# Linear attention of the second block's first layer over its context, made in steps between the experts' products

## The chip, the cores and the metric

The kernel runs on one core of a Trainium2 chip. The metric is the device time of one execution in microseconds (us). TensorE does the matrix products, VectorE and ScalarE the elementwise work, GpSimd (POOL) a few fills, and SyncE (SP) issues the large transfers from HBM.

## The reference, cut to what matters

Two transformer blocks run one after the other over 256 latent tokens of 1024 channels, in float32. The first block ends in a mixture of 32 experts. The second block has two layers; in each, the latents (`x`) and 256 context tokens (`ctx`) go through a hybrid mixer: retention and gated linear attention (GLA), each with 4 heads, both directions.

```python
h, hc = modulate_2(rmsnorm(x, ...)), modulate_2(rmsnorm(ctx, ...))
lat, cx = project_in(h, w_in), project_in(hc, w_in)
# GLA, for one direction: context scans from zero, latents from the context's last state
c_f, s_f = chunked_gated_linear_attention(cq, ck, cv, ca_f, zero, False)
x_f, _   = chunked_gated_linear_attention(q, k, v, a_f, s_f, False)
# merge: silu of a gate projection, then w_out and a squared-ReLU MLP, for x and (first layer) for ctx
```

The context of the second block (`ctx_2`) does not depend on the first block. In the first layer its outputs are needed (they go on to the second layer); in the second layer only its last states are.

## The kernel before

Matrix products of the mixers and the MLP split each float32 weight on the chip into a high and a low part: ScalarE rounds a 1 MB chunk to `whi` (`split`, L215), VectorE subtracts it to `wlo` (L216), and TensorE makes three products per tile of 128 x 128 (`mm3`, L226 to L228). The transposed activations stand in `hh` (high parts) and `hl` (low parts), 512 columns wide: columns 0 to 255 are the latents, 256 to 511 the context.

`moe` (the experts) walks over 16 pairs of experts. For each pair `q`, `gate_up` makes gate and up products (L1271) from 8 chunks of 1 MB, and `down` the down products (L1301) of pair `q - 1` from 4 chunks. These products are plain float32, 64 rows of each of two experts side by side in the array. `turned` transposes the hidden layer (L1286). Between the products, `step()` takes pieces from a list: the gathering of rows for the next four experts (`dispatch`, L1234 to L1248) and the adding of results (`combine`, L1319). `weights()` hands out chunks in the order of use, and `chunk(i)` gives each a buffer out of 14: three of the tag `raw` of `s.wp`, three of the tag `raw` of the local pool, the two `whi` and two `wlo` buffers, and four halves of `h0` and `h1`. A chunk's transfer is issued by SP, in order, when the buffer's last product has read it. At the end of `moe`, `context()` loads `ctx_2` and makes its inverse norms.

`block2` then runs the two layers. At the start of a layer, `values` makes the GLA values for all tokens, `proj` the gate's low-rank input, and, for each pair of heads `hp`, keys and queries; a loop over heads makes the decays and the GLA itself. Retention follows (from `vr`, with `proj(512...)`, L1654 on); last come the two gates (`proj_t`, with `sink`, L1733 to L1747), the transposes into `yh`, `yl`, `w_out` and the MLP. In the first layer (`need`), 512 columns are handled throughout; in the second, queries, decays and outputs are 256 wide, but the gate's input, keys and values still 512, and a separate scan (L1564, L1566) makes the context's last states. The modulation vectors of later parts (`ada`, VectorE, L287 and L289) are made in between, a piece at each `tick`.

All engines run their own queues in order. The order in each queue is made when the kernel is built: a planner takes instructions by their place in the program, and moves a ready one ahead of one that it expects to wait; `issue_after` pins a few places. Buffers of a tag are given out as they come free.

## Time and profile before

| what | us |
|---|---|
| median of 3 runs (lowest to highest) | 2022.29 (2019.41 to 2023.18) |
| the profiled execution, its own time | 2024.16 |
| its span, first to last instruction | 2022.0 |
| TensorE busy in the span | 1935.8 |
| VectorE, ScalarE busy | 1136.2, 693.1 |

The experts' stage takes about 415 to 895 us of the span, the first layer of the second block about 895 to 1600 us, and the second layer the rest. "Busy" of TensorE counts modelled ends of pipelined products, so that a high share alone does not say that it runs at its peak; intervals between the starts of like products do. Times are read from one profiled execution.

### The profile page before, as it was taken

The numbers are of one execution on the slowest core, as the hardware profiler recorded it, in microseconds if no ns is written. First come the engines' busy times: TensorE is split into PE (matmuls) and PEld (weight loads), VectorE is DVE, ScalarE is ACT, GpSimd is POOL, SyncE is SP. The second block draws the span as 40 slices with busy tenths as digits, with TensorE's granted clock in tenths as the row PEclk, the third lists the DMA queues.
The fourth block names the chain that finished last, engine by engine and source line by source line (L and its number), as shares of the span: only waits on it lengthen the run. The fifth ranks groups of instructions, "written<-read, shape, count | busy, mean of one in ns | idle before, by whom it ended". The sixth has DMA issues, their size and how long they took to land.

```text
span 2022.0 us, 27853 instructions
## 1 busy us (share of the span) xinstructions
PE 1935.8 (96%) x11540; PEld 1451.0 (72%) x11540; DVE 1136.2 (56%) x2110; ACT 693.1 (34%) x1023; POOL 5.4 (0%) x14
## 2 busy tenths in 40 slices
PE   6998999999999999989899999999999989999998
PEld 2866779844444444357778989778788967988998
DVE  5768795521111111144879959655634667887555
ACT  2564543421111111144432334131323444444444
POOL 0000000000000000000000000000000000000000
PEclk9999999999999999989799999999999989999999
DMA  8436536889999999953133424444423143467553
GB/s 292 161 105 208 167 130 228 310 360 421 420 421 421 421 421 421 421 203 114 43 126 125 148 83 137 155 146 137 134 84 104 56 149 113 151 203 229 176 180 104
DMA packets 218074, 426.15 MB, mean 211 GB/s; under 512 B 16428, under 2 KB 152585, under 8 KB 193113
## 3 DMA queue, kind: packets, MB, share of 16 engines
q1 hardware_dynamic: 208616, 419.75, 57.3%
q10 hardware_dynamic: 9200, 4.51, 0.8%
q8 instruction: 92, 1.51, 0.3%
q14 instruction: 38, 0.30, 0.0%
q0 software_dynamic: 128, 0.08, 0.0%
HBM read 423.26 MB, written 1.05 MB: 210 GB/s over the span
## 4 chain that ended last, share of the span: by engine, by line
PE 66%; DVE 6%; DMA 4%; ACT 2%; issue 1%; DVEq 0%; ACTq 0%; SPq 0%
PE mm L226 14%; PE mm L227 14%; PE mm L228 14%; PE mm L1271 9%; PE mm L1301 3%; PE at L1301 3%; DMA raw<-in_moe_w_down_dram 2%; PE at L1234 2%; PE tr L296 1%; PE at L1319 1%; DMA raw<-in_moe_w_up_dram 1%; DVE wlo L216 1%; DMA rawh<-in_moe_w_gate_dram 1%; DVE sx L1620 1%; DVE acc L289 1%
## 5 line engine op out<-in xcount | busy, mean ns | idle before, releaser
L228 PE MATMUL mm<-hh,wlo 128*128 128x256 f32 (+2 forms) x1232 | 405.7, 330 | 9.2 <-DVE wlo L216 9.2
L226 PE MATMUL mm<-hh,whi 128*128 128x256 f32 (+2 forms) x1232 | 409.9, 333 | 2.8 <-ACT hh L220 1.5
L227 PE MATMUL mm<-hl,whi 128*128 128x256 f32 (+2 forms) x1232 | 407.2, 331 | 0.1
L216 DVE TENSOR_TENSOR wlo<-raw,whi 128x2048 fp32r<-128x2048 f32 (+2 forms) x138 | 303.7, 2200 | 166.0 <-ACT whi L215 165.9
L215 ACT CAST whi<-raw 128x2048 fp32r<-128x2048 f32 (+2 forms) x138 | 253.1, 1834 | 357.9 <-PE mm L227 297.8
L228 PEld LDWEIGHTS mm<-hh,wlo 128*128 128x128 f32 (+1 forms) x1232 | 235.6, 191 | 33.7 <-DVE wlo L216 10.7
L226 PEld LDWEIGHTS mm<-hh,whi 128*128 128x128 f32 (+1 forms) x1232 | 235.6, 191 | 29.3 <-issue 3.6
L227 PEld LDWEIGHTS mm<-hl,whi 128*128 128x128 f32 (+1 forms) x1232 | 235.4, 191 | 25.8 <-issue 5.4
L289 DVE SCALAR_TENSOR_TENSOR acc<-raw,sc,acc 128x512 f32<-128x512 f32 x308 | 218.9, 745 | 14.5 <-DMA raw<-in_ada_w_dram 13.0
L226 PE MATMUL mm<-hidh,whi 128*128 128x256 f32 (+1 forms) x544 | 178.8, 331 | 0.0
L227 PE MATMUL mm<-hidl,whi 128*128 128x256 f32 (+1 forms) x544 | 177.5, 329 | 0.0
L228 PE MATMUL mm<-hidh,wlo 128*128 128x256 f32 (+1 forms) x544 | 177.1, 329 | 0.1
L1271 PE MATMUL mm<-raw,xg 128*64 128x512 f32 x736 | 172.5, 595 | 1.2 <-DMA raw<-in_moe_w_up_dram 1.2
L226 PE MATMUL mm<-whi,hh 128*128 128x256 f32 x512 | 152.9, 299 | 4.7 <-ACT vr L1518 2.9
L227 PE MATMUL mm<-wlo,hh 128*128 128x256 f32 x512 | 151.0, 295 | 3.4 <-DVE wlo L216 3.4
L228 PE MATMUL mm<-whi,hl 128*128 128x256 f32 x512 | 151.7, 297 | 0.7 <-DVE hl L371 0.7
L1271 PEld LDWEIGHTS mm<-raw,xg 128*64 128x64 f32 x736 | 54.6, 137 | 98.0 <-issue 93.0
L1279 DVE SCALAR_TENSOR_TENSOR glo<-mm,ws,glo 128x512 f32<-128x512 f32 x16 | 12.0, 751 | 191.0 <-PE mm L1271 169.0
L227 PEld LDWEIGHTS mm<-hidl,whi 128*128 128x128 f32 x544 | 102.3, 188 | 10.5 <-DVE hidl L221 0.6
L228 PEld LDWEIGHTS mm<-hidh,wlo 128*128 128x128 f32 x544 | 101.7, 188 | 11.1 <-DVE wlo L216 0.7
L226 PEld LDWEIGHTS mm<-hidh,whi 128*128 128x128 f32 x544 | 101.8, 188 | 11.0 <-ACT hidh L220 0.7
L226 PEld LDWEIGHTS mm<-whi,hh 128*128 128x128 f32 x512 | 102.7, 201 | 9.6 <-ACT vr L1518 3.8
(506 smaller groups left out, 2720.2 us busy)
## 6 DMA issues: line engine op xcount, KB each, us to landing
raw<-in_ada_w_dram SPq DMA_DIRECT2D x68, 1024.0 KB, 5.3
raw<-in_w_mlp_dram SPq DMA_DIRECT2D x64, 1024.0 KB, 5.3
raw<-in_w_in_dram SPq DMA_DIRECT2D x48, 1024.0 KB, 5.2
raw<-in_moe_w_down_dram SPq DMA_DIRECT2D x48, 1024.0 KB, 16.7
raw<-in_moe_w_gate_dram SPq DMA_DIRECT2D x46, 1024.0 KB, 13.8
raw<-in_moe_w_up_dram SPq DMA_DIRECT2D x46, 1024.0 KB, 15.5
rawh<-in_moe_w_gate_dram SPq DMA_DIRECT2D x18, 1024.0 KB, 13.1
rawh<-in_moe_w_up_dram SPq DMA_DIRECT2D x18, 1024.0 KB, 12.4
```

Source lines behind the costliest of these rows:

```text
L215: self.nc.scalar.copy(hv, v)
L216: self.nc.vector.tensor_tensor(lv, v, hv, op=OP.subtract)
L226: mt(out, ah, bh, start=first, stop=False)
L227: mt(out, ah, bl, start=False, stop=False)
L228: mt(out, al, bh, start=False, stop=last)
L289: nc.vector.scalar_tensor_tensor(acc[:, i], v[:, kk], s[:, k:k + 1], acc[:, i], op0=OP.mult, op1=OP.add)
L296: nc.tensor.matmul(pt[:n, :P], self.hot[:, 15 - r:15 - r + n], acc[:, r // 4, (r % 4) * P:(r % 4 + 1) * P], start=r == 0, stop=r == n - 1)
L1234: mt(px, tk[:, a, k * P:(k + 1) * P], sel[:, a], start=tk is th and a == 0, stop=tk is tl and a == 1)
L1271: mt(pg[64 * j:64 * j + 64], xg[:, k, 2 * i + j], vs[j][:, kk], start=k == 0, stop=k == 7)
L1301: mt(pd[c][sl], hT[:, k, sl], vs[j][:, kk, 512 * c:512 * c + 512], start=k == 0, stop=k == 3)
L1319: mt(po[:, j], y[:, i, sl], selT[:, i], start=y is yh and i == 0, stop=y is yl and i == 1)
L1620: nc.vector.scalar_tensor_tensor(sxs[ps_, b_], sxs[ps_, a_], etot[ps_, a_:a_ + 1], adds[a_][ps_], op0=OP.mult, op1=OP.add)
```

## The change

The GLA of the first layer over the context, from the norm to the gated output, moves into `moe`. `context()` becomes a generator of 37 steps and a last piece; after each of the four steps of `gate_up`, from `q = 1` on, one is taken (`next(ctx, None)`). It loads `ctx_2`, transposes and modulates it into `hc` (which takes the place of `h1`), loads and splits nine chunks of `w_in_2`, makes values, gate input, keys, queries, the four heads (four steps each) and the output gates, and leaves the gated outputs in `s.yc` and the last states in `s.cst`. What is left of it at `q = 16` would run there at once. The experts' chunks have less room: 8 buffers at first, then two halves of `h0`, then a ring of 6 (three `raw` of `s.wp`, which the context's chunks use as well, one `raw` of the pool and the two halves), and for the last 8 chunks a ring of 4. `block2` takes `hc` as `hl`, with the context's high parts copied to the right half of `hh`; in its first layer GLA then handles 256 columns and starts from `s.cst`, and `s.yc` is read in the transposes. The same weights are loaded and split a second time there. `ctx_2` is loaded again for the residual, and the small GLA parameters too (`gla_params`, now a function of its own). Some tags get fewer buffers.

```diff
-        pool = Pool(pool_, {"b8": 5, "b4": 3, "s4": 4, "t2": 6, "sq": 3,
+        pool = Pool(pool_, {"b8": 4, "b4": 3, "s4": 4, "t2": 6, "sq": 3,
...
-        pool = Pool(pool_, {"xg": 2, "raw": 3, "sel": 2, "selT": 3, "hT": 2, "ws": 3, "glo": 3, "sq": 4},
+        pool = Pool(pool_, {"xg": 2, "raw": 1, "t1": 4, "kq": 4, "sel": 2, "selT": 3, "hT": 2, "ws": 4, "glo": 2, "sq": 2},
...
-        slots = [(s.wp, "raw")] * 3 + [(pool, "raw")] * 3 + [(s.wp, "whi"), (s.wp, "wlo")] * 2
+        first = [(s.wp, "raw")] * 3 + [(pool, "raw")] + [(s.wp, "whi"), (s.wp, "wlo")] * 2
         big = []
 
         def chunk(i):
-            n = i % (len(slots) + 4)
-            if n < len(slots):
-                p_, tag = slots[n]
+
+            if i >= 8:
+                n = 4 + (i - 8) % 2 if i < 10 else (i - 10) % 6 if i < 184 else (i - 184) % 4
+            if i < 8 or n < 4:
+                p_, tag = first[i if i < 8 else n]
                 t = p_.tile([P, 2048], F32, tag=tag, name="raw")
             else:
 
-                if len(big) < 2:
-                    big.extend(s.xp.tile([P, 2, 2048], F32, tag=f"h{h}", name="rawh") for h in range(2))
-                t = big[(n - len(slots)) // 2][:, n % 2]
+                if not big:
+                    big.append(s.xp.tile([P, 2, 2048], F32, tag="h0", name="rawh"))
+                t = big[0][:, n - 4]
             src = s.expert_w(*order[i])
             v = t.rearrange("p (k c) -> p k c", k=src.shape[1])
             nc.sync.dma_start(v, src)
             return v
 
 
-        pre = s.pre + [chunk(i) for i in range(3, len(slots))]
-        made = len(slots)
+        pre = s.pre + [chunk(i) for i in range(3, 8)]
+        made = 8
...
                     step()
+                    if q > 0:
+                        next(ctx, None)
...
+        def load_context():
+            s.ctx2 = s.raw(I["ctx_2"][0].rearrange("(a p) d -> p a d", p=P))
...
+            load_context()
+            kb = pool.tile([P, 512], F32, name="kbc")
+            nc.scalar.dma_start(kb, I["k_b2"][:, 0:512])
+            maskF, maskB, rs64 = kb[:, 0:128].bitcast(I32), kb[:, 128:256].bitcast(I32), kb[:, 256:512]
+            gng, upst, gb = gla_params(s, pool, 0)
+            am = pool.tile([P, 2, P], F32, name="amc")
+            nc.gpsimd.memset(am, 0.0)
+            yield
+            cs = pool.tile([P, 2, 2], F32, name="cs")
...
+            hc = s.hc = s.xp.tile([P, 8, 512], F32R, tag="h1", name="hc")
+            for k in range(0, 8, 2):
+                pt = s.tr((P, 2, 2, P))
+                for kk in range(2):
+                    for a in range(2):
+                        nc.tensor.transpose(pt[:, kk, a], s.ctx2[:, a, (k + kk) * P:(k + kk + 1) * P], s.ident)
...
+            hh, hl = hc[:, :, :T], hc[:, :, T:]
+            yield
+            cols = [(2560, 256), (2816, 256), (3584, 32)]
+            for hp in range(2):
+                cols += [(2304 + 128 * hp, 128), (2048 + 128 * hp, 128)]
+            cols += [(3072, 256), (3328, 256)]
+            raws = [s.raw(w2[:, :, c:c + n]) for c, n in cols[:1]]
+
+            def weights_c():
+
+                w = s.split(None, raws.pop(0))
+                cols.pop(0)
+                if cols:
+                    raws.append(s.raw(w2[:, :, cols[0][0]:cols[0][0] + cols[0][1]]))
+                return w
+
+            def product(w, m):
+                pt = s.mm()
+                for k in range(8):
+                    s.mm3(pt[:m, :T], w[0][:, k, :m], w[1][:, k, :m], hh[:, k], hl[:, k], k == 0, k == 7)
+                return pt
...
+            vg = pool.tile([P, 2, 512], F32, name="vgc")
+            for c in range(2):
+                w = weights_c()
+                for a in range(2):
+                    nc.scalar.copy(vg[:, a, 256 * c:256 * c + 256], product_t(w, a))
+                    yield
+            dT = pool.tile([32, T], F32, name="dTc")
+            nc.scalar.copy(dT, product(weights_c(), 32)[:32, :T])
+            yc = s.yc = s.cp.tile([P, 2, 4, P], F32, name="yc")
+            cst = s.cst = s.cp.tile([P, 4, P], F32, name="cst")
...
+            for hp in range(2):
+                kst2, qst2 = [[pool.tile([P, T], F32, tag="kq", name=n) for _ in range(2)] for n in ("kst", "qst")]
+                yield
+                pt = product(weights_c(), P)
+                for j in range(2):
+                    for d in range(2):
+                        nc.scalar.copy(kst2[j][64 * d:64 * d + 64], pt[64 * j:64 * j + 64, :T])
...
+                for j in range(2):
+                    h = 2 * hp + j
+                    kst, qst = kst2[j], qst2[j]
+                    pg = s.tr()[:, :T]
+                    mt(pg, upst[:, h], dT, start=True, stop=True)
+                    bcol = gb[:, h:h + 1]
+                    c1, c2 = t1("c1"), t1("c2")
...
+                    nc.scalar.copy(ket, pt[:, :2])
+                    pas = [s.at((P, 4, P)) for _ in range(2)]
...
+                            to = cst[ps_, h] if i == 3 else sxs[ps_, a_ + 1 - 2 * d]
+                            nc.vector.scalar_tensor_tensor(to, sxs[ps_, a_], etot[ps_, a_:a_ + 1],
+                                                           pk[a_ % 2][ps_, a_ // 2], op0=OP.mult, op1=OP.add)
...
+                    nc.scalar.copy(yc[:, :, h], po[:, :2])
...
+            for c in range(2):
+                w = weights_c()
+                for a in range(2):
+                    g = t1("g", [P, 2, P])
+                    nc.scalar.activation(g, product_t(w, a).rearrange("p (h v) -> p h v", h=2), AF.Silu)
...
+        ctx = context()
...
-                context()
+                for _ in ctx:
+                    pass
+                load_context()
+                s.hh2 = s.xp.tile([P, 8, 512], F32R, tag="h0", name="hh2")
+                nc.scalar.copy(s.hh2[:, :, T:], s.hc[:, :, :T].bitcast(F32))
...
-        hh = s.xp.tile([P, 8, 512], F32R, tag="h0", name="hh")
-        hl = s.xp.tile([P, 8, 512], F32R, tag="h1", name="hl")
+        hh, hl = s.hh2, s.hc
...
-        s.norm_mod(pool, c2T, s.md2[3], s.md2[1], hh[:, :, T:], hl[:, :, T:], r=s.rc2)
...
+            GW = T if need else 512
+            vg = values(2560, "vg", (0,) if need else (0, 2))
+            pd, = proj(3584, n=GW, width=32)
...
-                pt, = proj(2304 + 128 * hp, width=128)
+                pt, = proj(2304 + 128 * hp, n=GW, width=128)
...
-                pt, = proj(2048 + 128 * hp, n=TW, width=128)
+                pt, = proj(2048 + 128 * hp, n=T, width=128)
...
-                    if not need:
+                    sxs = pool.tile([P, 4, P], F32, tag="sx", name="sx")
+                    if need:
+                        nc.gpsimd.tensor_copy(sxs[:64, 0], s.cst[:64, h])
+                        nc.gpsimd.tensor_copy(sxs[64:, 3], s.cst[64:, h])
+                    else:
...
-                    proj_t(c0 + 256 * c, NT, sink)
+                    proj_t(c0 + 256 * c, 2 if kind else NT, sink)
...
-                        nc.tensor.transpose(pt[:, h], o[:, a, h], s.ident)
+                        nc.tensor.transpose(pt[:, h], s.yc[:, a - 2, h] if kind and a > 1 else o[:, a, h], s.ident)
...
-        pool = Pool(pool_, {"b8": 5, "t2": 12, "nt": 3, "sx": 2, "rm": 1, "etot": 2, "st": 4},
-                    {"sq": "t2", "acc": "b8"})
+        pool = Pool(pool_, {"b8": 5, "t2": 12, "sx": 2, "rm": 1, "etot": 2, "st": 4},
+                    {"sq": "t2", "acc": "b8", "nt": "t2"})
```

## Rows read from the trace of the kernel before

**Rows 1.** The page: busy us, share of the span, instructions of each engine.

```profile
PE 1935.8 (96%) x11540; PEld 1451.0 (72%) x11540; DVE 1136.2 (56%) x2110; ACT 693.1 (34%) x1023; POOL 5.4 (0%) x14
```

**Rows 2.** Windows, experts' stage: length; busy (count) by engine; clock, DMA share, GB/s.

```profile
500.00:600.00 100.00, 99.82 (x482) 42.32 (x479) 13.40 (x38) 14.58 (x33) 0.00 (x0) 1.00 1.01 421
...
830.00:878.00 48.00, 44.67 (x195) 17.68 (x195) 7.02 (x13) 5.50 (x9) 0.00 (x0) 1.00 1.01 412
```

**Rows 3.** The chain that ended last, experts' stage: start, length, what.

```profile
609.84 1.64 PE at L1319 x11
...
645.63 13.79 PE mm L1271 x64
...
669.05 1.64 PE at L1319 x11
...
796.17 17.61 DMA rawh<-in_moe_w_gate_dram
```

**Rows 4.** Waits of SP's queue, 450 to 850 us: in total, times, longest.

```profile
SPq L1148 <- PE mm L1271: 146.3, 62, 7.1
```

**Rows 5.** The page's DMA issues: count, size, us from issue to landing.

```profile
raw<-in_ada_w_dram SPq DMA_DIRECT2D x68, 1024.0 KB, 5.3
```

**Rows 6.** The chain, start of layer 0: one product, 256 and 512 columns wide.

```profile
907.36 0.12 PE mm L226
...
939.85 0.23 PE mm L227
```

**Rows 7.** Windows, first layer of the second block (columns as in rows 2).

```profile
900.00:943.00 43.00, 42.96 (x265) 37.54 (x265) 22.21 (x45) 17.33 (x33) 0.00 (x0) 0.93 0.34 100
943.00:1034.00 91.00, 78.88 (x508) 66.11 (x508) 74.66 (x149) 38.09 (x68) 0.52 (x1) 0.83 0.19 62
1034.00:1160.00 126.00, 126.00 (x834) 112.04 (x833) 113.66 (x256) 40.95 (x52) 0.00 (x0) 1.00 0.46 152
```

**Rows 8.** Timeline of ScalarE: first queries' and first retention keys' copies, both layers.

```profile
943.90 2.41 ACT L1539 ACTIVATE qst<-mm 64x512 f32<-64x512 f32 x4
...
1039.94 0.59 ACT L1654 COPY ks<-mm 128x512 f32<-128x512 f32 x1 [2.09 <-PE mm L228]
...
1631.99 1.55 ACT L1539 ACTIVATE qst<-mm 64x256 f32<-64x256 f32 x4
...
1707.91 0.59 ACT L1654 COPY ks<-mm 128x512 f32<-128x512 f32 x1 [0.45 <-PE mm L228]
```

**Rows 9.** Groups by form, GLA heads, first layer, then second: busy, mean ns.

```profile
L1620 DVE SCALAR_TENSOR_TENSOR sx<-sx,etot,at 64x128 f32<-64x128 f32 x56 | 19.4, 347 | 4.1 <-PE at L1608 2.5
...
L1620 DVE SCALAR_TENSOR_TENSOR sx<-sx,etot,at 64x128 f32<-64x128 f32 x24 | 8.3, 346 | 2.6 <-PE at L1608 1.8
...
L1564 DVE TENSOR_TENSOR_SCAN e<-ones,c 64x255 f32<-64x255 f32 x4 | 2.7, 680 | 0.1
```

**Rows 10.** The chain, second layer: one head's products, 256 tokens (L1545: 512).

```profile
1680.30 1.06 PE tr L1545 x2
...
1695.73 0.22 PE tr L1599 x2
...
1696.70 0.69 PE at L1608 x8
...
1699.38 0.68 PE at L1629 x4
...
1701.43 0.64 PE at L1635 x4
1702.07 0.59 PE at L1639 x8
```

**Rows 11.** Groups by form, 1625 to 1715 us: splits of a chunk, a table load.

```profile
L215 ACT CAST whi<-raw 128x2048 fp32r<-128x2048 f32 x5 | 9.5, 1899 | 4.7 <-PE mm L227 4.6
...
L216 DVE TENSOR_TENSOR wlo<-raw,whi 128x2048 fp32r<-128x2048 f32 x4 | 9.2, 2289 | 0.4 <-ACT whi L215 0.4
...
L312 ACT ACT_TABLE_LOAD x1 | 1.3, 1283 | 0.0
```

## What was predicted

> **What bounds the kernel now.** I read the page first: TensorE is busy for 1935.8 of 2022.0 us, VectorE for 56%, ScalarE for a third [rows 1]. TensorE's busy time holds modelled ends, so I asked each of the two stages that the change touches what ends last there.
>
> The experts' stage: in windows of it TensorE is busy for 99.82 of 100 us at the full clock, and the transfers take all of the DMA engines' time at 421 GB/s [rows 2]. Which of the two is late? The chain runs from product to product, with no step through a transfer, until 796 us; only then does it pass through one [rows 3]. Two pairs of experts take 669.05 - 609.84 = 59.2 us, 29.6 per pair [rows 3]. The 64 gate and up records of a pair take 13.79 us, 0.215 each, and stand one right behind the other [rows 3], so this is no modelled tail: TensorE is full. The transfers need 12 chunks of 1.049 MB at 421 GB/s, 29.9 us per pair. Both are full, and TensorE has been ahead only by the stock of 14 buffers. SP waits for products to free buffers, 146.3 us in all [rows 4].
>
> The first layer of the second block, up to 1160 us, has three stretches [rows 7]. From 900 to 943 products follow without a gap. From 943 to 1034 the heads run: TensorE is busy for 78.88 of 91 us at a granted clock of 0.83, which means parts of it at 1.2 GHz after it had waited, and VectorE for 74.66. This stretch is set by chains through VectorE, not by products. From 1034 to 1160 TensorE has no gap, and VectorE is busy for 113.66 of 126.
>
> **What the layer saves.** Products that go: values 96 and output gates 96 of 256 columns, at 0.12 us, 11.5 us each; the gate's input 24, keys and queries 96 of 512 columns that become 256, 0.23 - 0.12 = 0.11 each, 13.2 us [rows 6]; and half of the heads.
>
> First stretch: the values (11.5) and those of the gate's input and the first pair's keys and queries (72 x 0.11 = 7.9) go from gapless work: 19.4 us. The context's norm that goes too lay beside these products: 0. Splits of ScalarE and VectorE stay and now have less product time over them; a 128-column chunk has half of a 256-column one's 1.9 and 2.29 us [rows 11] against 24 x 0.12 = 2.9 us of products, still covered.
>
> Middle stretch: from the first pair's query copies to retention's first keys it takes 1039.94 - 943.90 = 96.0 us. The second layer does the same with 256 tokens in 1707.91 - 1631.99 = 75.9 us [rows 8], and has work that the changed layer won't have: a 512-wide key product (24 x 0.11 = 2.6), two scans per head (8 x 0.68 = 5.4, rows 9), and multiplies and copies of the same kind, which I take as half as much again. That leaves an estimate of some 63 us and a saving of 33. Bounds: 20, as in the second layer, and 48, half. The state updates alone, 56 x 0.347 against 24 x 0.346 [rows 9], are 11.1 us of it.
>
> Last stretch: 11.5 us of gate products go, but VectorE, with 12 us free in 126, has the same splits and modulation vectors to make in a shorter time. Between 0 and 11.5; I take 7, nearer to the products that set it now.
>
> GpSimd gets eight copies of 64 x 128 that the trace doesn't show. Their data are old and GpSimd is idle [rows 1]: 0; if a head waited for them, a VectorE operation of that shape has 0.35 us [rows 9], 2.8 in all.
>
> Sum: 19.4 + 33 + 7 = 59 us saved, bounds 39 and 79.
>
> **What the experts' stage gains in work.** 312 products of 256 columns (values 96, gate input 24, keys and queries 96, output gates 96) at 0.12: 37.4 us. A head: L1545 at half of 1.06 = 0.53, two transposes 0.22, L1608 0.69, L1629 eight records at up to 0.17 = 1.36, L1635 0.64, L1639 0.59 [rows 10]: 4.0 us, 16.1 for four. Sixteen transposes of `ctx_2`, which the layer goes on doing for the residual, at 0.11: 1.8. Together 55 us, in a stage whose TensorE is full. It is about what leaves the layer (11.5 + 11.5 + 13.2 + 16 = 52): the work moves from one full engine to the same full engine.
>
> Hidden are: nine splits and the heads' elementwise work (VectorE and ScalarE are busy for 14 of 100 us in the stage, rows 2), and the table loads between exponentials and the experts' silu, 1.28 us each [rows 11], at most two per pair. These operations are long, though, and the transposes of `turned` wait for VectorE's multiply just ahead of them: behind a `wlo` of 2.29 us they come later by up to that. The Trainium skill (ScalarE: Activation LUTs, "Table sets: the hidden batching unit" and "What ACT_TABLE_LOAD costs") says to batch activations by set, which the change does not, and puts a switch at 2.66 us; its 1.28 for the load alone agrees with the row, the rest no row here shows. By it twenty switches would be 53 us of ScalarE, which had 85 of 100 us free, and the sum would stay.
>
> Transfers: 8.5 MB of weights, 1 MB of `ctx_2` and small constants are (9.8 MB)/(421 GB/s) = 23 us more. With TensorE at 35 us per pair for the nine pairs that carry steps (37 steps, four a pair) and the transfers at 29.9 + 2.6 = 32.5, this is hidden, if the buffers let the transfers run ahead.
>
> Do they? They fall from 14 to 6, and one of these holds a chunk of the context at times; SP is in order, so the experts' chunks stand behind a context chunk that waits for a `raw` buffer, and TensorE behind them. A chunk alone lands in 5.3 us [rows 5], of which 2.5 are its bytes at 421 GB/s, so two chunks land 7.8 us after their buffers come free. TensorE eats two in 13.79 / 4 = 3.45 us when products stand back to back. With three pairs of buffers full at the start of a `gate_up`, the fourth is there at 3.45 + 7.8 = 11.25 and wanted at 10.35: 0.9 us late; the two of `down` are 1.5 late each. If other work fills the latter, it is 0.9 per pair of experts, else 3.9: 9 to 35 us over nine pairs. I take 10, near the lower end, since the program puts a step of the context behind every two chunks, and 2 for the ring of 4 at the end: 12.
>
> The buffers taken from block 1 (`b8`) and in the layer (`nt` among `t2`) cost nothing: in block 1 at most four tiles of that tag are wanted at once, and the norm's tiles live before the heads begin.
>
> **The sum.** 55 + 12 - 59 = +8 us on the execution's own 2024.16. This lies 1.9 above the median of the runs, so I forecast 2030 us, slower by 0.4%. Alone, this case spans 2024 to 2045. A measurement of this kernel can tell 0.2%, 4 us.
>
> **Rivals.**
> 1. Faster: the heads' stretch is a chain, and half the elements halve it. Then the layer saves 19.4 + 48 + 11.5 = 79, and the stage, with the context's products standing where TensorE would wait for chunks, takes 55 to 60: 2024 - 20 = 2004, or some 2010 in between. It decides as soon as the layer saves over 67. For it: VectorE's work there is near its length, 74.66 of 91. Against: the second layer, most of whose operations have half the columns, still takes 75.9 us [rows 8].
> 2. Nothing: saving and cost meet, with the stage at 57 to 62: 2018 to 2026.
> 3. Starved: nothing fills the late chunks, or a context chunk keeps its `raw` buffer for a whole `gate_up`. 35 + 5 instead of 12 gives 55 + 40 - 59 = +36, 2057. For it: today's stock of 14 buffers is drained by 796 us [rows 3] although the engines match; against: with the steps TensorE is slower than the transfers.
> 4. The stage has room. TensorE's weight loads are busy for only 42 of 100 us there [rows 2]; if the rest were room, the 55 us would be free and only the saving left: 2022 - 59 = 1963 us. The 0.215 us between records speaks against it [rows 3]. This is what the Trainium skill would read (Perfetto Trace Analysis, "Identifying the Most-Contended Engine"): not matmul busy time but weight-load busy share tells headroom; its next section even advises to interleave regimes with different bounds. By the row, both regimes have the same bound here.
>
> That the steps don't spread, because the planner moves them or `q = 16` takes the rest, changes little: 38 calls are needed and 60 are there, and wherever they stand in the stage they cost the same products.
>
> **Chances.** Forecast 0.42, faster (1) 0.27, nothing (2) 0.14, starved (3) 0.14, room (4) 0.03. Faster: 0.27 + 0.03 = 0.30; same: 0.14 and a little of the forecast's lower edge, 0.15; slower: 0.55. The range goes from rival 1's better end, 2004, to 2060, where starving with the middle saving ends; it leaves out case 4 and the ends of 1 and 3.
>
> **What the changed profile would show.** Pairs 1 to 9 of the experts at some 36 us instead of 29.6, TensorE busy all through, transfers under 400 GB/s in these pairs; the stage ending 65 to 70 us later; from the first value product to retention's keys some 52 us less. The step of the buffers is wrong if the later pairs, without steps, stay at 29.6 and TensorE never waits for a chunk; the 33 us is wrong if query copies to retention's keys differs from 63 us by more than 6. The prediction is wrong on the whole if the heads' stretch falls below 55 us, or if pairs with steps take over 40.

## The result and the profile after

The changed kernel takes 2096.73 us (median of 4, 2095.14 to 2100.45), the kernel before 2021.66 beside it: a ratio of 1.0375 (95% interval 1.0356 to 1.0394), 75 us slower. The forecast was 2030, its range ended at 2060. The direction (slower) was right; the size was not.

Where the time went can be read from the starts of each pair's multiply into `glo` on VectorE. From the first to the last of sixteen it is 421.6 us before (437.3 to 858.9) and 551.5 after (437.5 to 989.0): the experts' stage grew by 130 us, where the forecast had 67. From the last one to the end of the span it is 1163.1 before and 1104.4 after: the layer gave 58.7, where the forecast had 59. So the whole miss lies in the stage. Its first ten intervals, the pairs with steps, took 39.9 us each (437.5 to 836.3), not 36. Before, the same ten took 28.1 each (281.4 in all), not the 29.6 that the forecast read from two of them. So these ten grew by 117 us, and the last five, without steps, by 12.6 (152.7 instead of 140.1).

Windows of the changed kernel, columns as in [rows 2]: pairs with steps, the last pairs without, the heads' stretch of the layer.

```profile
463.50:836.30 372.80, 346.92 (x1737) 169.57 (x1736) 95.76 (x226) 98.92 (x183) 1.20 (x6) 0.97 0.85 327
836.30:988.90 152.60, 141.46 (x651) 58.29 (x650) 21.48 (x41) 16.53 (x32) 0.00 (x0) 1.00 0.99 404
1020.50:1117.60 97.10, 87.75 (x582) 77.26 (x583) 74.88 (x156) 44.20 (x96) 4.11 (x12) 0.83 0.43 132
```

Before, TensorE was busy for 99.82 of 100 us in the stage and the transfers ran at 421 GB/s [rows 2]. Now TensorE has 26 us without work in 373, the granted clock is 0.97 (stretches at 1.2 GHz), and the transfers run at 327 GB/s: neither is full. Even the pairs without steps have 11 us of gaps. Their waits, TensorE's through the stage and SP's from 450 to 850 us (what waited, for whom, in total, times, longest):

```profile
PE mm L1287 <- DMA raw<-in_moe_w_up_dram: 11.9, 6, 3.7
PE tr L1496 <- DVE de L1490: 11.5, 4, 4.6
PE mm L1287 <- DMA rawh<-in_moe_w_up_dram: 6.2, 6, 1.3
```

```profile
SPq L1164 <- PE mm L1287: 145.4, 42, 13.8
...
SPq L1164 <- DVE wlo L216: 41.2, 8, 14.7
```

TensorE waits for chunks, and four times, once per head, at the transposes of `de`. SP's queue has a wait that [rows 4] had not: `wlo`, the end of a split, for 41.2 us. An expert's chunk stands there for a buffer that a context chunk holds until it is split, and all later chunks stand behind it. SP's timeline shows one such place: after a context chunk (L175) at 513.81 the two `up` chunks behind it took SP until 528. TensorE has no gap in these 16 us (last line, a window with columns as in [rows 2]), but the transfers run at 248 GB/s instead of 421, so the stock of chunks shrinks there.

```profile
513.81 0.38 SPq L175 DMA_DIRECT2D raw<-in_w_in_dram  x1
514.62 13.54 SPq L1164 DMA_DIRECT2D raw<-in_moe_w_up_dram  x2
528.25 0.86 SPq L1164 DMA_DIRECT2D rawh<-in_moe_w_up_dram  x2
...
513.80:530.00 16.20, 16.20 (x86) 9.06 (x85) 4.35 (x9) 1.82 (x4) 0.00 (x0) 1.00 0.69 248
```

Each head's wait is a chain of short operations. ScalarE's timeline beside one head, then TensorE's, then the window behind it:

```profile
594.28 0.47 ACT L1468 ACTIVATE c<-tr,gb 128x256 f32<-128x256 f32 x1 [0.28 <-PE tr L1465]
594.77 1.28 ACT L1470 ACT_TABLE_LOAD   x1
596.07 0.42 ACT L1470 ACTIVATE c<-c 128x256 f32<-128x256 f32 x1
596.50 1.28 ACT L1471 ACT_TABLE_LOAD   x1
597.79 0.51 ACT L1471 ACTIVATE c<-c,ones 128x256 f32<-128x256 f32 x1
598.32 1.28 ACT L1489 ACT_TABLE_LOAD   x1
601.10 0.42 ACT L1489 ACTIVATE de<-de 128x256 f32<-128x256 f32 x1 [1.50 <-DVE de L1484]
```

```profile
602.03 0.44 PE L1496 MATMUL tr<-kres,de 128*128 128x128 f32 x2 [4.15 <-DVE de L1490]
602.40 1.95 PE L1319 MATMUL mm<-raw,hT 128*64 128x512 f32 x4
```

```profile
602.50:605.90 3.40, 3.40 (x9) 0.99 (x10) 0.42 (x1) 0.42 (x1) 0.00 (x0) 0.50 1.01 422
```

From the first operation of the chain to the transposes it is 7.8 us. Three table loads (loads of ScalarE's function tables) stand beside it, but only the first two, 2.6 us, lie on the chain: the third runs beside VectorE's scans, and ScalarE idles for 1.50 us behind it. TensorE stands for 4.15 us with products of `down` behind it in its order, and then runs at half the clock for 3.4 us.

In the layer the forecast's own sign came out: from the first query copies to retention's first keys it is 1117.65 - 1050.69 = 67.0 us, within 63 ± 6, against 96.0 before [rows 8].

```profile
1050.69 1.55 ACT L1727 ACTIVATE qst<-mm 64x256 f32<-64x256 f32 x4
...
1117.65 0.59 ACT L1839 COPY ks<-mm 128x512 f32<-128x512 f32 x1 [3.28 <-PE mm L228]
```

### The profile page after: what moved, and what is told of

It is laid out like the page before. It is cut to its first block, busy times and chain, and to the rows that moved or that the text cites. A ratio compares the mean times of both kernels' runs of the same rounds, so it can differ in the third digit from the quotient of the medians.

```text
span 2093.4 us, 28360 instructions
## 1 busy us (share of the span) xinstructions
PE 1973.5 (94%) x11684; PEld 1460.8 (70%) x11684; DVE 1156.8 (55%) x2161; ACT 742.1 (35%) x1117; POOL 9.9 (0%) x32
## 4 chain that ended last, share of the span: by engine, by line
PE 44%; DVE 4%; ACT 2%; issue 0%; DMA 0%; DVEq 0%; ACTq 0%
PE mm L226 13%; PE mm L227 13%; PE mm L228 13%; PE tr L296 1%; DVE wlo L216 1%; PE at L1893 1%; PE at L1887 0%; DVE nt L366 0%; DVE hc L371 0%; ACT whi L215 0%; DVE acc L289 0%; DVE sx L1805 0%; PE tr L1850 0%; PE at L1879 0%; PE at L1897 0%
## 5 line engine op out<-in xcount | busy, mean ns | idle before, releaser
L216 DVE TENSOR_TENSOR wlo<-raw,whi 128x2048 fp32r<-128x2048 f32 (+2 forms) x147 | 318.2, 2164 | 183.2 <-ACT whi L215 183.0
L227 PE MATMUL mm<-hc,whi 128*128 128x256 f32 (+2 forms) x952 | 314.1, 330 | 0.2
L228 PEld LDWEIGHTS mm<-hh,wlo 128*128 128x128 f32 (+1 forms) x1232 | 235.3, 191 | 31.0 <-DVE wlo L216 10.7
L289 DVE SCALAR_TENSOR_TENSOR acc<-raw,sc,acc 128x512 f32<-128x512 f32 x308 | 219.2, 745 | 14.2 <-DMA raw<-in_ada_w_dram 12.7
L227 PEld LDWEIGHTS mm<-hc,whi 128*128 128x128 f32 (+1 forms) x952 | 180.5, 190 | 18.3 <-issue 2.6
L1287 PE MATMUL mm<-raw,xg 128*64 128x512 f32 x544 | 144.7, 620 | 14.2 <-DMA raw<-in_moe_w_up_dram 11.9
L226 PE MATMUL mm<-whi,hh 128*128 128x256 f32 x448 | 134.2, 300 | 5.3 <-ACT vr L1704 2.7
L1287 PE MATMUL mm<-rawh,xg 128*64 128x512 f32 x480 | 131.0, 598 | 7.7 <-DMA rawh<-in_moe_w_up_dram 6.2
L227 PE MATMUL mm<-wlo,hh 128*128 128x256 f32 x448 | 132.5, 296 | 5.3 <-DVE wlo L216 5.3
L228 PE MATMUL mm<-whi,hc 128*128 128x256 f32 x448 | 133.7, 299 | 1.8 <-DVE hc L371 1.8
L1287 PEld LDWEIGHTS mm<-raw,xg 128*64 128x64 f32 x544 | 42.1, 142 | 89.0 <-issue 66.5
L227 PE MATMUL mm<-hl,whi 128*128 128x256 f32 (+1 forms) x320 | 100.0, 313 | 0.0
```

Of the source, the lines that this page charges most:

```text
L216: self.nc.vector.tensor_tensor(lv, v, hv, op=OP.subtract)
L226: mt(out, ah, bh, start=first, stop=False)
L227: mt(out, ah, bl, start=False, stop=False)
L228: mt(out, al, bh, start=False, stop=last)
L289: nc.vector.scalar_tensor_tensor(acc[:, i], v[:, kk], s[:, k:k + 1], acc[:, i], op0=OP.mult, op1=OP.add)
L1287: mt(pg[64 * j:64 * j + 64], xg[:, k, 2 * i + j], vs[j][:, kk], start=k == 0, stop=k == 7)
```

## The experiments

Three theories of the missing time: **A**, the chunks come late (six buffers, shared with the context's chunks); **B**, the heads' chains make TensorE stand, with the half clock behind it; **C**, the products cost more than they last. Ratios are against the kernel before, run beside each. Its medians there lie between 2020.47 and 2023.13, so that a difference of two rows can be off by some 2.7 us; the single times scatter most in `one_set` (2083.0 to 2096.4) and `heads12` (1997.3 to 2009.2).

| run | us | ratio, 95% interval |
|---|---|---|
| ring_only | 2055.74 | 1.0162 (1.0142 to 1.0181) |
| ring14_layer | 1961.51 | 0.9712 (0.9695 to 0.9728) |
| ring12_layer | 1967.19 | 0.9734 (0.9718 to 0.9750) |
| ring6_layer | 1998.31 | 0.9894 (0.9877 to 0.9910) |
| no_heads_loads | 2046.63 | 1.0132 (1.0115 to 1.0149) |
| no_heads | 2069.22 | 1.0228 (1.0208 to 1.0247) |
| no_loads | 2083.52 | 1.0297 (1.0269 to 1.0325) |
| few_products | 2090.17 | 1.0332 (1.0311 to 1.0353) |
| heads12 | 2005.94 | 0.9911 (0.9885 to 0.9938) |
| heads12_spaced | 1983.99 | 0.9814 (0.9798 to 0.9831) |
| heads6 | 2028.80 | 1.0036 (1.0023 to 1.0049) |
| heads6_spaced | 2009.90 | 0.9938 (0.9921 to 0.9955) |
| spaced_one_table | 2095.41 | 1.0366 (1.0349 to 1.0383) |
| one_set | 2090.15 | 1.0327 (1.0302 to 1.0353) |
| wide | 2097.06 | 1.0362 (1.0344 to 1.0380) |
| mended | 2081.04 | 1.0301 (1.0284 to 1.0318) |
| late | 2096.56 | 1.0370 (1.0350 to 1.0390) |
| norm_only | 2032.54 | 1.0050 (1.0038 to 1.0062) |

### The buffers and the layer, each alone

Of the kernel before, with the changed kernel's `chunk` (six buffers) and nothing else:

```diff
-            n = i % (len(slots) + 4)
+            if i >= 8:
+                n = 4 + (i - 8) % 2 if i < 10 else (i - 10) % 6 if i < 184 else (i - 184) % 4
```

> The kernel before, with nothing of the change but the smaller set of buffers for the experts' chunks (six instead of fourteen in turn, four at the end); no step of the context stands in the stage, the layer computes everything as before. Three theories of the 62 us that the forecast missed. Starved chunks (A): the smaller set, and its sharing with the context's own chunks, starves TensorE; the pairs without steps lost 12.6 us over five, so at that rate fifteen pairs lose 38 us: 2060 us. Chains of the heads (B): TensorE stands in its order behind transposes that wait for ScalarE's and VectorE's chain with its table loads, and is slowed after each stand; then the ring costs what the last pairs show at most: 2022 to 2035 us. Dearer work (C): the products cost more than their durations where they stand between the experts' float32 products: 2022 to 2035 us here. The forecast had 12 us for this part: 2034 us.

It took 33 us more, near A's 38 and nearly three times the forecast's 12.

Of the changed kernel, with `context()` left out; its results are constants, and the chunks have 14, 12 or 6 buffers:

```diff
-        ctx = context()
+            s.yc = s.cp.tile([P, 2, 4, P], F32, name="yc")
+            s.cst = s.cp.tile([P, 4, P], F32, name="cst")
...
+        ctx = iter(())
...
+                s.hc = s.xp.tile([P, 8, 512], F32R, tag="h1", name="hc")
```

> The second block's layer over the latents alone, with the kernel before's fourteen buffers in the experts' stage and no step of the context in it: the context's rows, state and normalized copy are constants, so the output is not the reference's. What the layer saves by itself. If the 54 us that the two traces showed behind the stage are the layer's alone: 2022 - 54 = 1968 us; the forecast's term of 59 us would give 1963 us. If part of those 54 us was time that the stage only passed on (a start with fuller buffers, weights that were already there): 1975 us or more.

> The layer over the latents alone and no step in the stage (constants for the context's results, so the output is not the reference's), with twelve buffers for the experts' chunks. By a straight line between fourteen (1961.5 us) and six (1998.3 us): 1971 us. If the price begins only where a pair's twelve chunks no longer fit: 1962 to 1965 us.

> As the kernel with the layer alone, but with the changed kernel's six buffers. If the ring's price and the layer's saving add up: 2056 - 54 = 2002 us, and the steps of the context are then worth 2097 - 2002 = 95 us in the changed kernel, of which their products' durations are some 58. If the price of the ring stood in the layer's start: nearer to 1968 us.

The layer saves 2020.5 - 1961.5 = 59.0 us by itself, and the buffers take from that: two fewer cost 5.7 us, eight fewer 36.8. The run with twelve lies between its two expectations. Windows of the stage with fourteen, then with six:

```profile
500.00:800.00 300.00, 299.51 (x1439) 129.05 (x1436) 44.62 (x104) 41.46 (x91) 0.00 (x0) 1.00 1.01 421
```

```profile
500.00:800.00 300.00, 287.92 (x1363) 122.29 (x1364) 41.57 (x99) 39.05 (x87) 0.00 (x0) 1.00 0.98 399
```

With six, 12 us of 300 are gaps; the waits behind them are nearly all for `up` and `down` chunks, many and short, 22.0 us in the stage. The stage is 36.4 us longer (457.0 instead of 420.6). Gaps are counted from modelled ends, so the waits can be more than they show; the rest is not resolved. SP, on its side, waits longer for the products of `gate_up` to free a buffer: 192.0 us instead of 144.6 from 450 to 850 us (`mm`; six, then fourteen).

```profile
PE mm L1287 <- DMA rawh<-in_moe_w_up_dram: 11.6, 12, 1.4
PE mm L1319 <- DMA raw<-in_moe_w_down_dram: 6.2, 8, 1.8
```

```profile
SPq L1164 <- PE mm L1287: 192.0, 85, 7.4
```

```profile
SPq L1162 <- PE mm L1285: 144.6, 62, 6.9
```

Two full engines wait for each other in turns, and with six buffers neither has the stock to go on meanwhile. The stock shows once more at the end: from the multiply of pair 13 to that of pair 14, beside which there is no dispatch, it is 22.4 us with fourteen buffers, 22.6 with twelve and 30.2 with six. With six, TensorE has 5.9 us of gaps in it, and 30.2 us is about what 12 chunks take at 421 GB/s (29.9). The Trainium skill (Perfetto Trace Analysis, "Optimization Strategy") says that the same bubble returning on the engine that should be full can mean too few buffers; these rows are such a case.

### Parts taken out of the changed kernel

Heads left out (results set to constants), loads left out (the splits read the token buffer `th`, save the 32 columns of the gate's input), or both; and products cut to k = 0:

```diff
-                    pg = s.tr()[:, :T]
-                    mt(pg, upst[:, h], dT, start=True, stop=True)
...
+                    nc.gpsimd.memset(cst[:, h], 0.0)
```

```diff
-                w = s.split(None, raws.pop(0))
+                return s.split(None, raws.pop(0) if n == 32 else thv[:, :, :n])
```

```diff
-                for k in range(8):
+                for k in range(1):
```

> The changed kernel without the four heads over the context: decays, scans, transposes, state and retention products are left out and their results set to constants; the projections with their loads and splits stay, and as many steps. So the output is not the reference's. The heads' own TensorE work is worth some 8 us. A and C: 2085 to 2090 us. B: the waits of the chains and the half clock after them go too, 40 us or more: 2035 to 2050 us.

> The changed kernel, but the context's weights are not loaded, save those of the 32 columns of the decays: the splits read the dispatch's token buffer instead, in the same shapes, so no chunk of the context takes one of the experts' six buffers or stands in SP's queue; 6.4 MB less to move, 6.3 MB of it in the stage. The numbers are therefore not the reference's. A: the starvation in the pairs with steps goes, by up to 45 us: 2050 to 2060 us. B and C: TensorE's work and the chains are all there: 2080 to 2097 us.

> The changed kernel with neither the heads over the context nor the loads of the context's weights (the splits read the dispatch's token buffer), so the output is not the reference's; normalization, splits and the 312 products stay. If the parts add up (chains of the heads 27.5, loads 13): 2097 - 40 = 2056 us. If starved chunks are one thing that either part keeps alive (a late chunk anywhere stops both queues), both together give more than the two apart: 2045 us, which is the 2002 us of ring and layer and the products' 37 us and some switches, with no stall at all.

> The changed kernel with one eighth of the context's projection products (k = 0 alone): 273 of the 312 products are left out, so the output is not the reference's; loads, splits, copies, heads and steps stay. 273 x 0.12 us = 33 us of TensorE work less. C, and any theory in which TensorE is full through the pairs with steps: 2097 - 33 = 2064 us or less (less if each product costs more than its duration there). A: chunks come too late whatever TensorE does, so little of it comes back: 2085 to 2097 us. B: the heads' chains stay as long, TensorE has less to fill them with: 2070 to 2085 us.

Of the expectations, `no_heads` fell between both readings, its 8 us for the heads' work being half of the forecast's 16.1. `no_loads` lies outside A's range, `few_products` inside it. `no_heads_loads` came near the 2045 us of one loss that either part keeps alive, not the 2056 of parts that add up.

Along one path, from the whole: the heads 27.5 us, then the loads 22.6, then norm, splits and products 48.3 (2046.63 - 1998.31), then the buffers 36.8, and 1961.5 is left. These are terms in this order only; against the kernel before beside each run, the heads are 29.0 and the loads 19.9. The loads alone are worth 13.2, and seven eighths of the products, 33 us of TensorE's time, just 6.6: while heads and loads hold things up, products fill gaps that stay without them. TensorE's waits in the run with few products:

```profile
PE mm L1287 <- DMA raw<-in_moe_w_up_dram: 26.9, 8, 6.5
PE tr L1496 <- DVE de L1490: 10.8, 3, 4.6
```

The first was 11.9 us with all products. So C falls as an explanation of the whole, and so does a TensorE that is full all through the pairs with steps; in the run without heads and loads, though, TensorE is full but for what six buffers cost (22.4 us of gaps in the stage, 23.1 in ring6_layer), and there norm and products cost what they last, some 9 us more than 37.4 + 1.8. Most of that can be read from its trace: the stage is 46.3 us longer than in ring6_layer; the 312 products take 40.7 us to the start of the next, 0.13 each and not 0.12; the norm's transposes and sums take 2.3; and two stretches at a granted clock of 0.5, 6.8 us in all, which ring6_layer has not, cost an estimated half of that. The loads show in SP's waits for the splits, without heads, with and without loads. How much of their cost is this wait and how much their bytes (6.4 MB, an estimate of 15 us at 421 GB/s) no run separates.

```profile
SPq L1164 <- DVE wlo L216: 34.5, 7, 9.6
```

```profile
SPq L1164 <- DVE wlo L216: 5.1, 1, 5.1
```

### The heads alone

The kernels with the layer alone, and the heads in the stage on constant keys, queries, values and decays; then with two more steps ahead of the transposes:

```diff
                     nc.vector.tensor_tensor(cu, cu, kst, op=OP.mult)
                     yield
+                    yield
+                    yield
                     pt = s.tr((P, 4, P))
```

> As the run with twelve buffers, with the four heads' steps in the stage, on constant keys, queries, values and decays (no projections, loads or splits, so the output is not the reference's). The heads' 128 products took 18 us by their spacing. If their loss beyond that is for want of cover: 18 to 24 us more than with twelve buffers and no steps, 1983 to 1990 us. If it is their own stands and the half clock behind them: 35 us more or above, 2000 us.

> As the run beside it with the changed kernel's six buffers: heads on constants, and nothing else of the context (so the output is not the reference's). Want of cover: 1998 + 37 = 2035 us, where the run with twelve pays the work alone. Their own stands: 2033 us or more as well, but then the one with twelve pays as much. If the heads lose only beside the projections' products and splits: 1998 + 18 to 22 = 2016 to 2020 us.

> The run with the heads alone on constants and twelve buffers, with two more steps between each head's decays and the transposes that wait for them (the output is not the reference's). If the stands and the half clock behind them are the loss: 11.6 us and half of 13.7 us come back, 2006 - 18 = 1988 us, no more than the work and some switches above the 1967 us without heads. If the time turns into another wait whatever the buffers: 2000 us or more.

> The same edit with six buffers (heads alone, on constants; the output is not the reference's). If the stands come back here too: 2029 - 18 = 2011 us. If with six buffers TensorE, sooner at its place, only waits longer for the next chunk: 2020 to 2029 us, which would say that the stands and the chunks' waits are paid once between them, and why the whole kernel did not gain by the same edit.

With twelve buffers the heads cost 38.7 us, with six 30.5: the loss is their own and needs no starved chunks (a lack of cover would have cost more with six). TensorE's wait there, with twelve, and a window behind one of the stands:

```profile
PE tr L1436 <- DVE de L1430: 11.6, 4, 4.6
```

```profile
562.30:569.20 6.90, 5.80 (x13) 1.83 (x14) 0.98 (x3) 1.66 (x4) 0.00 (x0) 0.51 0.72 303
```

Two more steps remove both (with twelve buffers no wait for `de` remains in the stage and no stretch below the full clock), and the heads cost 16.8 us with twelve buffers, their work as forecast (16.1), and 11.6 with six, where part of the work, some 5 us, seems to fill waits for chunks (15.0 us of gaps in the stage, 23.1 in ring6_layer). B is shown for this part.

### The order of the whole kernel's steps

One more step ahead of the transposes, with a single table set that took no effect (three loads for each head remained); then the set loaded in place; then one step more and the set, with another step ahead of seven of the nine splits (`wide`); then the set with two more steps ahead of the transposes (`mended`). The expectations count 40 steps in the changed kernel; there are 37, with 49 in `wide` and 45 in `mended`.

```diff
+                    with tc.issue_after(last_):
+                        set_ = nc.scalar.preload_act_table_set("natural_log_exp_and_others").ins
...
+                    with tc.issue_after(set_):
+                        nc.scalar.activation(c1, pg, AF.Abs, bias=bcol)
```

> The changed kernel, complete, with two edits of each head over the context: the table set that holds the exponential and the logarithm together is loaded ahead of the decays (one load of 1.28 us for a head instead of three), and one more step lies between the decays' chain and the transposes that wait for it. Chains of the heads (B): the 26 us that TensorE stood for VectorE's product of the decays go, and the half clock behind them with it: 2060 to 2072 us. Starved chunks (A): the time returns as waits for chunks: 2085 to 2097 us.

> The changed kernel, complete, with the table set that holds exponential and logarithm loaded once for each head, this time held in ScalarE's order behind the head's last copy before it (in the run before the load was placed where it had no effect, and the three loads for each head stayed). It takes away two to three of the 1.28 us loads of each head, some 10 us of ScalarE. If the heads' chain through ScalarE sets the pairs' length (B): 2097 - 10 = 2087 us or less. If not: 2093 to 2100 us.

> The changed kernel, complete, with the one set as in the run beside it, one more step between the decays' chain and the transposes that wait for it, and one more step ahead of each split of the context's weights, so that the chunk has landed when its split comes up on ScalarE and VectorE; the 40 steps become about 54 of the 60 places there are. Stops in order (D: an instruction of a step, above all a split that waits for its transfer, stands ahead of the pair's own copies on ScalarE and VectorE, and what TensorE waits for comes late): 2060 to 2080 us. If only the six buffers matter: 2090 to 2100 us, since each context chunk holds one of the six for longer.

> The changed kernel, complete, with two more steps between each head's decays and its transposes and the table set of exponential and logarithm loaded once for each head (48 steps of the 60 places). If the heads' stands are lost on their own, as with the heads alone: 2097 - 19 = 2078 us. If beside the context's loads and splits the next chunk comes no sooner, so that TensorE only stands elsewhere: 2088 to 2097 us. The heads' whole part was 27.5 us, of which 17 are work, so not below 2080 by the first reading's own row. Faster than the kernel before it cannot be by either.

One step more shortened the stands at `de` from 11.5 to 4.6 us (the 26 us of its expectation count the same stands twice, for products and for weight loads) and lengthened the waits for `up` chunks by as much:

```profile
PE mm L1287 <- DMA raw<-in_moe_w_up_dram: 19.1, 7, 5.0
...
PE tr L1499 <- DVE de L1492: 4.6, 1, 4.6
```

One set gave 6.6 us by the medians, with 17 table loads in the stage instead of 20, but one of its four times is 2096.4, so this gain is uncertain; two more steps and the set gave 15.7 us with 23 loads. So the number of loads alone does not set the time. That a load costs where TensorE stands at the end of its chain fits these runs, but none isolates it. `wide` gained nothing, and why is not settled; nor is why one step more gave nothing where two gave nearly the 19 us that they gave with six buffers and the heads alone.

All steps in one stretch behind the last pair:

```diff
-                    if q > 0:
-                        next(ctx, None)
```

> The changed kernel with all 40 steps made in one stretch behind the last pair's products, none between the pairs. The stage then costs what the six buffers cost (1998 us with the layer alone), and the context's work stands alone: 58 us of TensorE's work, four bare chains of some 8 to 10 us, transfers and splits ahead of the products: 2090 to 2110 us. If the steps between the pairs hide at least the chains, as the change would have it, the changed kernel's 2097 us is the lower one by 20 us or more: 2117 us or more.

It took as long as the changed kernel (2096.56 and 2096.73 us). Put between the experts' products, the steps gain nothing on balance over one stretch at the end. In one stretch they are far from free themselves; here is a window of it, with TensorE at a granted clock of 0.71 and gaps of 14 us in 40:

```profile
960.00:1000.00 40.00, 26.34 (x157) 20.42 (x157) 29.24 (x77) 23.08 (x49) 1.19 (x6) 0.71 0.12 36
```

The smallest part alone, on the kernel before: norm and transposes in the stage, twelve buffers, the layer over 512 columns.

```diff
-            n = i % (len(slots) + 4)
+            n = i % (len(slots) + 2)
...
+                    if q > 0:
+                        next(ctx, None)
...
-        s.norm_mod(pool, c2T, s.md2[3], s.md2[1], hh[:, :, T:], hl[:, :, T:], r=s.rc2)
```

> The kernel before with the smallest part of the change: the context's rows are transposed, normalized and split between the experts' products in pairs 1 and 2 (16 transposes, some 2 us of TensorE's work, one load of 1 MB), and everything else stays in the layer over 512 columns; the normalized copy takes the room of two of the fourteen buffers. The layer's first stretch then loses what the forecast gave it, 19 us. If buffers are worth 33 to 37 us for eight, two are worth up to 9 us, at once or by degrees: 2022 - 19 + 2 + 0 to 9 = 2005 to 2014 us. If the stage cannot take even these steps (a stop on either queue is lost on both): 2020 us or more.

It is 10 us slower. The stage grew by 16 us (437.9 instead of 421.6 from first to last `glo`), the part behind it shrank by 9 (1154.2 instead of 1163.1). Two buffers fewer had cost 5.7, and the transposes are some 2. The rest can be read from the transfers: SP waits once for 11.3 us until the context's rows, whose chunk holds a `raw` buffer, are transposed, and the transfers run at 342 and 351 GB/s until 505, where the kernel before has 420 from 440 to 500. TensorE has no gap in these windows, but an estimated 12 us of transfers are missing afterwards, enough for the rest. The pair without dispatch takes 29.8 us here, 22.4 before.

```profile
SPq L1148 <- PE tr L1372: 11.3, 1, 11.3
```

```profile
437.00:470.00 33.00, 33.00 (x176) 14.30 (x173) 8.16 (x23) 8.28 (x16) 0.00 (x0) 1.00 0.84 342
470.00:505.00 35.00, 35.00 (x193) 18.05 (x193) 10.68 (x29) 7.90 (x18) 0.00 (x0) 1.00 0.86 351
```

The 19 us of the expectation were my slip: in the forecast they belong to the products of the first stretch, which this run keeps. No version that was run with the steps complete beats the kernel before.

## Why the prediction was right on the side and wrong on the size

- **The layer, 59 us:** measured 59.0 alone and 58.7 in the changed kernel's trace. By stretches, from the last `glo` to the first query copies, to retention's first keys and to the end, it gave 23.3, 29.1 and 6.4 us where the forecast had 19.4, 33 and 7. The norm that it set to nothing is worth 9 us by the smallest run, and lies in the first stretch, so that the products there gave some 14 instead of 19.4: part of the sum's precision is luck.
- **The work, 55 us:** heads 16.8 for 16.1; products, norm and splits 48.3 for 39.2. The premise, that the work moves from a full TensorE to a full TensorE, held: once heads and loads are out, moving it gains nothing. A product's time was a little too small, 0.13 us in the stage against 0.12 [rows 6]. Rival 4, room in TensorE, would have had 1963 us, as if the steps were free: ring14_layer's time, which has no steps. The Trainium skill's rule (Perfetto Trace Analysis, "Identifying the Most-Contended Engine"), to judge TensorE's headroom by its share of peak work and by its weight loads' busy share, would have misled by the latter: at a share of 0.42 the work that was added cost all of its time.
- **The buffers, 12 us: the step that failed first.** Measured 36.8, near rival 3's 35 + 5. By the traces of the runs with fourteen and six, 22.2 us of it lie in the first ten pairs and 14.2 in the last five. The forecast had 10 for the pairs with steps, the lower end of its 0.9 to 3.9 us a pair, where it is 2.2, and only 2 for the rest, where all five pay. The wait that it worked out is there: TensorE waits 12 times for `up` chunks in the halves of `h0`, the fourth pair of `gate_up`, 0.97 us on average against 0.9. What it had wrong is how many pairs pay, and that nothing else would be late: `down` waits 8 times, 6.2 us, and the pair without dispatch is 7.8 us longer (30.2 against 22.4). It took one chunk's landing from [rows 5], 5.3 us; with six buffers the page of the kernel with the layer alone has 4.9 to 9.6 us, which may be a part of it:

```profile
raw<-in_moe_w_down_dram SPq DMA_DIRECT2D x64, 1024.0 KB, 7.6
...
raw<-in_moe_w_gate_dram SPq DMA_DIRECT2D x34, 1024.0 KB, 4.9
raw<-in_moe_w_up_dram SPq DMA_DIRECT2D x34, 1024.0 KB, 5.6
rawh<-in_moe_w_gate_dram SPq DMA_DIRECT2D x30, 1024.0 KB, 9.6
```

  The reason for taking the lower end, that steps fill the late chunks, holds for some 5 us by the heads with six buffers; on balance `late` speaks against it.
- **The transfers, 0: the second.** "Hidden, if the buffers let the transfers run ahead": they did not, and the loads cost 22.6 us in the order above. The 23 us of transfers were too many: nine chunks of 1568 columns in all are 6.4 MB, not 8.5, so with `ctx_2` some 18 us. Rival 3 named both (a context chunk that keeps its buffer, 35 + 5), and had 14% of the chance; by buffers and loads, 59 us, it was right and still too small.
- **The elementwise chains and table loads, 0: the third.** They were set to nothing because VectorE and ScalarE were idle for 85 of 100 us [rows 2]. But TensorE's order puts each head's transposes behind a chain of 7.8 us, and `down` behind them. With twelve buffers and the heads alone this is 38.7 - 16.8 = 21.9 us; in the changed kernel `mended` gave 15.7, and in the order above it is 27.5 - 16.8 = 10.7, since without the heads TensorE waits longer for chunks (18.1 us instead of 11.9 for `raw` `up`).

Together: 24.8 for buffers, 22.6 for loads, 10.7 for chains and 9.1 for products make 67.2, against 66.7 missed, in that order of taking parts out. That they close proves nothing, since each is a difference of neighbours on one path; another order shares the miss out otherwise, and the loads alone are 13.2. The prediction's own signs of being wrong on the whole stayed silent, a heads' stretch below 55 us (67.0) and pairs with steps over 40 (39.9): against 28.1 before, 40 was far too wide a bound. The sign that should have decided was in the text too: when two engines are full beside each other [rows 2, 3], the stock between them is worth time by itself.

## What to carry to other kernels

Where a stage keeps TensorE and the transfers full at once, buffers are not spare room: price them by a run with fewer buffers and nothing else. A chain on idle engines is hidden only if TensorE's own order has enough work between its start and the product that waits; count that distance in us, not the engines' busy share. Moving TensorE work into a stage whose TensorE is full gains at best nothing, so the move needs another reason.

## What was unexpected in the hardware

A stand of 4.15 us was followed by 3.4 us at a granted clock of 0.50, and one of 4.16 us in the run with twelve buffers, which ended at 563.4, by a clock of 0.51 until 569.2. If half of the time behind them is lost, these stands cost, by estimate, 1.4 and 1.7 times their length. And leaving out 33 us of products let the mean clock of the stage fall from 0.98 to 0.96, while its gaps grew from 40.7 to 59.4 us: with less work the engine stood more, and ran slower behind the stands.
